# The MLP's down product by one level of Strassen's method, its operands summed in the up stage

## The chip, the cores and the metric

The kernel runs on one core of a Trainium2 chip. The metric is the device time of one execution in microseconds (us); three executions are given, with their median. One further execution was recorded by the hardware profiler, and all rows below are read from it. PE is TensorE, DVE VectorE, ACT ScalarE, POOL GpSimd, SP the sync engine, which here only issues DMAs; POOL issues DMAs too.

## The reference

One step of a small encoder: 1024 prompt frames and 64 sample frames, together T = 1088 columns, model width 1024, two layers. Layer 0 mixes tokens by attention, layer 1 by a gated linear recurrence. Each layer ends with

```python
def sqrelu_mlp(h, w_up, w_down):
    return jnp.square(jax.nn.relu(h @ w_up)) @ w_down
...
        yp = yp + sqrelu_mlp(rmsnorm(yp, mlp_norm[i]), mlp_w_up[i], mlp_w_down[i])
```

where `w_up` is 1024 x 4096 and `w_down` 4096 x 1024, all in float32. After the last layer stands one more rmsnorm.

## The kernel before

Columns are frames. The residual x is held transposed, as four tiles `pair0` to `pair3` of 128 x 2 x 1088 (eight rows of 128 features). A float32 product is made of three matmuls of fp32r operands: each number is split into a high part (a cast) and a low part (the difference), and high x high, high x low and low x high are summed (`product`, L117 to L119). For weights, `parts` makes the two halves: ACT casts (L107), DVE subtracts (L108); a raw weight tile is 128 x 512, that is four blocks of 128 x 128, 256 KB.

Stages in order of time: attention, up and down of layer 0 (`up`, `down`), recurrence, up and down of layer 1, final norm. The PE's order within a stage is written in the code; a scheduler sets the other engines' orders from it, each engine then works its own list strictly in order.

**Up** is already done by a Strassen level in Winograd's form. For each of 16 values of m it makes four pieces of the hidden matrix, 128 rows by half of the columns (544): y11 and y12 are row tile 2m, y21 and y22 are row tile 2m+1, each for the left and the right half of the columns. Seven products of 24 matmuls of 272 columns each (`mul`, L880) give them; weights are combined by `diff` (L925), products by `plus` (L892), `finish` squares (L886, L887) and stores each piece to DRAM (`y_mlp`, L888) through POOL's queue. Before this, the residual itself goes to DRAM (`x_mlp`, L913), so that its four tiles serve as work space.

**Down** takes the 32 hidden tiles in five groups (`GROUPS`), which alternate between two sets of buffers: e (`eh`, `el`, six tiles) and x (`xh`, `xl`, eight tiles). `hidden` loads a tile from `y_mlp` through POOL's queue (L963, 544 KB), ACT casts it (L964), DVE subtracts (L965). The residual comes back by L989 on SP's queue, as do the raw weights (L84). For each group, each of eight output tiles d, and each of three chunks of columns (364, 362, 362; in the last group of layer 1 416, 416, 256), `product` runs over the k tiles of the group and `mix_acc` (L443) adds the result to x.

The pools matter for what follows: the pool `up` holds, among others, the temporaries `d1`, `tt`, `q` and a raw tile of the up stage and is released at its end; the pool `down{layer}` is opened then, in the same memory. A tile of a pool that takes over memory waits until everything that used this memory, DMAs too, is over.

Of the kernel before, what the change touches and what calls it, by code (L numbers as in the profile page):

```python
# [8 lines left out]
F32 = mybir.dt.float32  # L9
# [8 lines left out]
P = 128  # L18
# [10 lines left out]
GROUPS = (4, 8, 6, 8, 6)  # L29
# [10 lines left out]
class Trunk:  # L40
# [717 lines left out]
    def operands(self, gi, ep, up):  # L758
        nc = self.nc
        eh, el = ([ep.tile([P, T], F32R, name=f"e{t}{i}", tag=f"e{t}{i}") for i in range(6)] for t in "hl")  # L760
# [66 lines left out]
    def up(self, ctx, layer, op, up):  # L827
        nc = self.nc
        pu = ctx.enter_context(self.tc.tile_pool(name=f"pu{layer}", bufs=4, space=PSUM))

        def acc():
            return pu.tile([P, 2, 512], F32, name="pu", tag="pu")[:, :, :TH // 2]
# [50 lines left out]
        def finish(t, j, a):  # L883
            y = room("y")
            r = self.rstd[:, TH * j:TH * j + TH]
            nc.vector.scalar_tensor_tensor(cols(y), a, 0.0, cols(r), ALU.max, ALU.mult)  # L886
            nc.scalar.activation(y, y, AF.Square)  # L887
            nc.gpsimd.dma_start(self.yk[layer][t, :, TH * j:TH * j + TH], y)  # L888
# [9 lines left out]
        self.half = None  # L898
# [17 lines left out]
        for t in range(2):  # L916
            for j in range(2):
                finish(t, j, ps[t][j])
# [9 lines left out]
        add, sub = nc.vector.tensor_add, nc.vector.tensor_sub  # L928
        for m in range(1, NF // 2):
# [15 lines left out]
            finish(tb, 1, plus("c", b4, s3))  # L945
            a12 = raw(ta, 1, up)
            mul(b1, self.parts(a12), "b21", True)
            finish(ta, 0, b1)
            mul(b3, self.parts(a22), "t4", True)
            finish(tb, 0, plus("c", b3, s2))  # L950
# [4 lines left out]
    def down(self, ctx, layer, final, ep):  # L955
        nc, tc, A = self.nc, self.tc, self.A
        self.banks(ctx, f"pd{layer}", 8)
        hp = ctx.enter_context(tc.tile_pool(name=f"down{layer}", bufs=1))
        self.CH = CH3

        def hidden(t, hh, hl):
            y = hl[:].bitcast(F32)
            nc.gpsimd.dma_start(y, self.yk[layer][t])  # L963
            nc.scalar.copy(hh[:], y)  # L964
            nc.vector.tensor_sub(hl[:], y, hh[:].bitcast(F32))  # L965
            return hh, hl

        def normed(c, ks):
            s, n = self.CH[c]
            for k in ks:  # L970
                y = hp.tile([P, 416], F32, name="y", tag="y", bufs=4)
# [4 lines left out]
        k0 = 0  # L976
        for g, n in enumerate(GROUPS):
            last = g == len(GROUPS) - 1
            hs = []
            for i in range(n):  # L980
                if g % 2:
                    h = self.xh[i], self.xl[i]
                else:
                    h = (ep.tile([P, T], F32R, name=f"e{t}{i}", tag=f"e{t}{i}") for t in "hl")
                hs.append(hidden(k0 + i, *h))
            if not g:
                self.xp = [self.pair(p) for p in range(4)]
                for p in range(4):
                    nc.sync.dma_start(self.xp[p][:], self.xk[layer][:, 2 * p:2 * p + 2, :])  # L989
            if last:  # L990
                self.new_norm()

            def part(d, into=None):
                return self.weight(A["w_down"][layer, d, :, k0:k0 + n, :], n, into)

            if last and final:
                self.CH, self.big = CHF, hp
                order = (6, 7, 0, 1, 2, 3, 4, 5)
                ws = {d: part(d, [t[i][:, :n * P].rearrange("p (n t) -> p n t", t=P) for t in (self.xh, self.xl)])
                      for d, i in zip(range(KT), order)}  # L1000
                for c in range(3):
                    for d in range(KT):
                        self.mix_acc(ws[d], hs, d, c)
                        done = self.square_part(d, c)
# [169 lines left out]
```

## Time and profile before

| | |
|---|---|
| median of three runs | 2516.59 us (2516.38 to 2516.81) |
| the profiled execution | 2516.2 us |
| its span, first to last instruction | 2514.2 us |
| up of layer 0, down of layer 0 | 397 to 739.6 us, 742.0 to 1124.0 us |
| up of layer 1, down of layer 1 | 1785 to 2114.9 us, 2117.6 to 2501.2 us |
| PE busy | 2471.4 us, 98% of the span |
| DVE, ACT, POOL busy | 59%, 39%, 6% |

The span is 2.0 us shorter than the profiled execution's time. A busy share is one over all stages; the stages differ, so what a change in one of them does has to be read in that stage.

### The profile page before, as it was taken

What the parts mean: (1) busy time and instruction counts of PE and PEld (TensorE: products, weight loads), DVE (VectorE), ACT (ScalarE), POOL (GpSimd) and SP (SyncE); (2) the same over time, 40 slices, a digit from 0 to 9 for tenths busy, and PEclk for the clock granted to TensorE, in tenths of its full rate; (3) what the DMA queues carried; (4) which work ended last, traced back from release to release, by engine and by line L of the source; (5) the groups of instructions that cost most, each with busy time, mean ns of one, the idle gap of its engine ahead of it and who ended that gap; (6) DMA issues with size and microseconds to landing.
All of it is one profiled execution on the core that took longest, in us unless ns stands there. A gap on an engine that the chain in (4) does not pass through costs nothing.

```text
span 2514.2 us, 43600 instructions
## 1 busy us (share of the span) xinstructions
PE 2471.4 (98%) x17704; PEld 2415.7 (96%) x17704; DVE 1485.5 (59%) x2781; ACT 974.3 (39%) x2045; POOL 161.1 (6%) x337
## 2 busy tenths in 40 slices
PE   8999999999999999999999999999999999999998
PEld 7998899999999999999999999999999999999997
DVE  7555458666674243267677777776866667324335
ACT  5236546333342022144555555544633334112122
POOL 2201100101120000000000000000011111000000
PEclk9999999999999999999999999999999999999999
DMA  5322132333363132131111011122233336312211
GB/s 166 85 56 67 38 104 85 108 104 104 104 240 129 43 115 98 42 127 35 38 38 38 29 38 38 32 101 102 92 104 105 104 104 251 104 58 98 104 55 72
DMA packets 108600, 223.39 MB, mean 89 GB/s; under 512 B 29024, under 2 KB 44000, under 8 KB 104672
## 3 DMA queue, kind: packets, MB, share of 16 engines
q1 hardware_dynamic: 85072, 138.84, 17.5%
q0 software_dynamic: 23328, 81.77, 8.8%
q8 instruction: 139, 2.28, 0.4%
q14 instruction: 61, 0.50, 0.1%
HBM read 158.95 MB, written 55.05 MB: 85 GB/s over the span
## 4 chain that ended last, share of the span: by engine, by line
PE 96%; DVE 1%; DMA 1%; ACT 1%; issue 1%; POOL 0%; SPq 0%; POOLq 0%; ACTq 0%; DVEq 0%
PE pu L880 24%; PE mm L117 20%; PE mm L118 19%; PE mm L119 19%; PE sc L331 2%; PE po L365 2%; PE pb L641 2%; PE pu L867 1%; PE pb L605 1%; PE pt L359 1%; PE pb L728 1%; PE pb L700 1%; PE pb L730 1%; PE pb L743 0%; PE pb L672 0%
## 5 line engine op out<-in xcount | busy, mean ns | idle before, releaser
L117 PE MATMUL mm<-xh,whi 128*128 128x384 f32 (+4 forms) x2208 | 731.2, 332 | 14.0 <-ACT whi L107 12.0
L118 PE MATMUL mm<-xl,whi 128*128 128x384 f32 (+4 forms) x2208 | 726.9, 330 | 0.0
L119 PE MATMUL mm<-xh,wlo 128*128 128x384 f32 (+4 forms) x2208 | 724.6, 329 | 0.0
L107 ACT CAST whi<-raw 128x512 fp32r<-128x512 f32 x352 | 197.5, 596 | 655.7 <-PE mm L118 547.8
L117 PEld LDWEIGHTS mm<-xh,whi 128*128 128x128 f32 x2208 | 416.9, 189 | 19.9 <-ACT whi L107 13.0
L443 DVE TENSOR_TENSOR pair<-pair,mm 128x362 f32<-128x362 f32 (+4 forms) x328 | 170.2, 525 | 433.3 <-PE mm L119 431.6
L118 PEld LDWEIGHTS mm<-xl,whi 128*128 128x128 f32 x2208 | 416.7, 189 | 3.5 <-issue 2.2
L119 PEld LDWEIGHTS mm<-xh,wlo 128*128 128x128 f32 x2208 | 416.8, 189 | 3.1 <-issue 1.2
L880 PE MATMUL pu<-xh,wlo 128*128 128x272 f32 x960 | 276.5, 288 | 0.0
L880 PE MATMUL pu<-xl,whi 128*128 128x272 f32 x960 | 275.6, 287 | 0.0
L880 PE MATMUL pu<-xh,whi 128*128 128x272 f32 x960 | 275.5, 287 | 0.0
L108 DVE TENSOR_TENSOR wlo<-raw,whi 128x512 fp32r<-128x512 f32 x352 | 222.5, 658 | 19.1 <-ACT whi L107 18.5
L117 PE MATMUL mm<-eh,whi 128*128 128x362 f32 (+1 forms) x624 | 205.0, 329 | 5.2 <-DVE pair L892 2.8
L880 PE MATMUL pu<-eh,wlo 128*128 128x272 f32 x720 | 208.0, 289 | 0.0
L880 PE MATMUL pu<-eh,whi 128*128 128x272 f32 x720 | 207.6, 288 | 0.4 <-DVE pair L892 0.4
L880 PE MATMUL pu<-el,whi 128*128 128x272 f32 x720 | 206.9, 287 | 0.0
L118 PE MATMUL mm<-el,whi 128*128 128x362 f32 (+1 forms) x624 | 204.7, 328 | 0.0
L892 DVE TENSOR_TENSOR pair<-pu,pair 128x544 f32<-128x544 f32 x150 | 108.5, 723 | 160.4 <-PE pu L880 159.6
L119 PE MATMUL mm<-eh,wlo 128*128 128x362 f32 (+1 forms) x624 | 203.1, 326 | 0.0
L880 PEld LDWEIGHTS pu<-xh,whi 128*128 128x128 f32 x960 | 180.9, 188 | 0.2 <-ACT whi L107 0.2
L880 PEld LDWEIGHTS pu<-xl,whi 128*128 128x128 f32 x960 | 180.5, 188 | 0.0
L880 PEld LDWEIGHTS pu<-xh,wlo 128*128 128x128 f32 x960 | 180.0, 188 | 0.0
(282 smaller groups left out, 4005.5 us busy)
## 6 DMA issues: line engine op xcount, KB each, us to landing
y_mlp<-pair POOLq DMA_DIRECT2D x128, 272.0 KB, 2.4
raw<-in_w_up SPq DMA_DIRECT2D x128, 256.0 KB, 2.7
raw<-in_w_down SPq DMA_DIRECT2D x112, 256.0 KB, 3.0
el<-y_mlp POOLq DMA_DIRECT2D x32, 544.0 KB, 7.2
xl<-y_mlp POOLq DMA_DIRECT2D x32, 544.0 KB, 8.3
raw<-in_w_in SPq DMA_DIRECT2D x64, 256.0 KB, 2.9
x_mlp<-pair SPq DMA_DIRECT2D x8, 1088.0 KB, 5.0
pair<-x_mlp SPq DMA_DIRECT2D x8, 1088.0 KB, 8.7
```

The costliest lines, as they stand in the source:

```text
L107: nc.scalar.copy(hi, raw)
L108: nc.vector.tensor_sub(lo, raw, hi.bitcast(F32))
L117: nc.tensor.matmul(ps[:, :n], wh, ih[:, s:s + n], start=i == 0, stop=False)
L118: nc.tensor.matmul(ps[:, :n], wh, il[:, s:s + n], start=False, stop=False)
L119: nc.tensor.matmul(ps[:, :n], wl, ih[:, s:s + n], start=False, stop=i == last)
L331: nc.tensor.matmul(ps[u][:, i, :kn], st, kd[g][r, k0:k0 + kn], start=True, stop=True)
L359: nc.tensor.transpose(pt[:, kt, :], pb[:, u, kt * P:(kt + 1) * P], self.ident[:])
L365: nc.tensor.matmul(out, ptts[u][:, kt, :], v, start=start, stop=stop)
L443: self.nc.vector.tensor_add(self.x(d)[:, s:s + n], self.x(d)[:, s:s + n], ps)
L641: nc.tensor.matmul(psa[r:r + 64 - hh, i // 2, :].rearrange("p (s t) -> p s t", t=hh), d[:, i * 64:i * 64 + 64 - hh], dv[:, i * ns:(i + 1) ...
L880: nc.tensor.matmul(ps[:, c, :], a, cols(b)[:, c, :], start=not more and p == i == 0, stop=p == 3 and i == 2, skip_group_check=True)
L892: nc.vector.tensor_tensor(t, ps, b, ALU.add)
```

## The change

Down, too, uses one level of Strassen's method. The weight matrix of an output pair m (output tiles 2m and 2m+1) and the hidden matrix are cut in two by rows and columns, b11 to b22 being the hidden quadrants (rows of tiles 2m, 2m+1; left and right columns). Seven products (`PRODS`) each take one combination of weight blocks and one of hidden quadrants and are added to or taken from one or two quadrants of the output. A product runs over all 16 k tiles for four output pairs, in matmuls of 272 columns; per layer 7 x 4 x 16 x 2 x 3 = 2688 matmuls instead of 2304.

The combined operands b21-b11, b21+b22, b11+b22, b12-b22 and b11+b12 are formed in the up stage (`mixed`, five DVE operations of 128 x 544 per m) and stored beside b11 and b22 (`keep`): seven stores of 272 KB per m instead of four. Down then loads 56 hidden tiles of 544 KB per layer instead of 32, forms the weight combination of five of the seven products by DVE (L1010), loads 192 raw weight tiles of 256 KB, and evacuates a product by additions of 128 x 544 (L1030). The PSUM pool of up and down is now one. The new raw tiles of second blocks and the tiles `q` are in `down{layer}` (here `hp`), so in memory that the pool `up` had.

```diff
+PRODS = (
+    (((1, 0), "+", (1, 1)), "b11", ((1, 0, "+"), (1, 1, "-")), ("e0", "e2", "x0", "x2")),
+    (((1, 1),), "b21-b11", ((1, 0, "+"), (0, 0, "+")), ("e4", "x4", "x6", "x0")),
+    (((0, 1), "-", (1, 1)), "b21+b22", ((0, 0, "+"),), ("e0", "e2", "x2", "x4")),
+    (((0, 0), "+", (0, 1)), "b22", ((0, 0, "-"), (0, 1, "+")), ("e4", "x0", "x6", "x2")),
+    (((0, 0), "+", (1, 1)), "b11+b22", ((0, 0, "+"), (1, 1, "+")), ("e0", "e2", "x4", "e4")),
+    (((0, 0),), "b12-b22", ((0, 1, "+"), (1, 1, "+")), ("x0", "x2", "x6", "x4")),
+    (((1, 0), "-", (0, 0)), "b11+b12", ((1, 1, "+"),), ("e0", "e2", "e4", "x0")),
+)
...
+        def mixed(p, f, na, a, sign, nb, b):
+            t = up.tile([P, TH], F32, name="d1", tag="d1", bufs=4)[:]
+            f(t, a, b)
+            self.keep(layer, na + sign + nb, p, t)
...
-            finish(ta, 1, plus("c", b4, s2))
+            y12 = finish(ta, 1, plus("c", b4, s2))
+            mixed(m, sub, "b12", y12, "-", "b22", y22)
+            mixed(m, add, "b11", y11, "+", "b12", y12)
...
+        def load(j, i):
+            (hs, ls), n = pair_of(PRODS[j][3][i])
+            for q, k in enumerate(n):
+                y = ls[k][:].bitcast(F32)
+                nc.gpsimd.dma_start(y, self.yk[layer][j, 2 * i + q].rearrange("p a n -> p (a n)"))
+                nc.scalar.copy(hs[k][:], y)
+                nc.vector.tensor_sub(ls[k][:], y, hs[k][:].bitcast(F32))
+
+        def raw(m, block, i, own):
+            r = self.raw() if own else hp.tile([P, 4, P], F32, name="raw", tag="raw", bufs=3)
+            nc.sync.dma_start(r[:], A["w_down"][layer, 2 * m + block[0], :, block[1], 4 * i:4 * i + 4, :])
+            return r[:]
+
+        def weights(a, m, i):
+            r = raw(m, a[0], i, True)
+            if len(a) > 1:
+                q = hp.tile([P, 4, P], F32, name="q", tag="q", bufs=2)[:]
+                nc.vector.tensor_tensor(q, r, raw(m, a[2], i, False), ALU.add if a[1] == "+" else ALU.subtract)
+                r = q
+            return self.parts(r)
...
+        for j, (a, name, outs, slots) in enumerate(PRODS):
+            end = j == len(PRODS) - 1
+            for m in range(4):
...
+                for i in order:
+                    last = mul(ps, weights(a, m, i), j, i, (0, 1), i == order[0], i == order[-1])
...
+                if j == 0:
+                    self.xp[m] = self.pair(m)
+                    if done:
+                        with tc.issue_after(done.ins):
+                            nc.sync.dma_start(self.xp[m][:], self.xk[layer][:, 2 * m:2 * m + 2, :])
...
+                evacuate(ps, m, outs)
+                if not end and m < 3:
+                    load(j + 1, m)
...
+            if not end:
+                load(j + 1, 3)
```

Where the up stage of layer 0 gives over to down, SP's queue stood as follows; `raw_8089`, `raw_8137` and so on are down's weights, `pair0_8031` to `pair3_8034` the residual, and the names in brackets are the semaphores waited for (DMASW: a DMA issued by POOL; DMAHW: one issued by SP).

```order
L84 DMA raw_8089<-in_w_down 128x512 [waits DMAHW7_49,DVE_49]
L84 DMA raw_8137<-in_w_down 128x512 [waits DMAHW5_49,DVE_49]
L989 DMA pair0_8031<-x_mlp0 128x2176 [waits DMASW3_49,DMASW2_49,DMASW4_49,DMASW1_49,Activation_49]
L84 DMA raw_8185<-in_w_down 128x512 [waits DMAHW1_49,DVE_49]
L989 DMA pair2_8033<-x_mlp0 128x2176 [waits DVE_49]
L84 DMA raw_8233<-in_w_down 128x512 [waits DMAHW4_49,DVE_49]
```

In the changed kernel the same place in SP's queue reads as follows; `raw_8240`, `raw_8272` and `raw_8306` are first blocks, `raw_8243` is the second block that belongs to `raw_8240`, `raw_8275` that of `raw_8272`.

```order
L1003 DMA raw_8272<-in_w_down 128x512 [waits DMAHW0_49,DVE_49]
L883 DMA raw_8101<-in_w_up 128x512 [waits DMAHW6_49,DVE_49]
L1003 DMA raw_8306<-in_w_down 128x512 [waits DMAHW5_49,DVE_49]
L1095 DMA pair0_8372<-x_mlp0 128x2176 [waits DMASW3_49,DMASW4_49,DVE_49,Activation_49]
L1093 DMA pair2_8658<-x_mlp0 128x2176 [waits DVE_49]
L1093 DMA pair3_8801<-x_mlp0 128x2176 [waits DVE_49]
L1093 DMA pair1_8515<-x_mlp0 128x2176 [waits DMASW3_49,DMASW1_49,DMAHW1_49,DVE_49,Activation_49]
L1003 DMA raw_8243<-in_w_down 128x512 [waits DMASW6_49,DMASW5_49,DMASW7_49,DMASW4_49,DMAHW2_49,DMASW3_49,DMAHW4_49,DMASW2_49,DMASW0_49]
L1003 DMA raw_8275<-in_w_down 128x512 [waits DMAHW3_49]
```

The first second block has moved behind all four loads of the residual, and it waits for seven DMAs of POOL's and two of SP's; among them, by their semaphores, are the stores of `d1_8166`, `d1_8169`, `d1_8205` and `d1_8208`, whose memory it takes.

POOL's queue of the changed kernel at this place is the following. `el` and `xl` are hidden tiles that are loaded for products 0 and 1, the `d1` tiles the combined operands of the last m.

```order
L997 DMA xl4_74<-y_mlp0 128x1088
L997 DMA xl5_75<-y_mlp0 128x1088
L997 DMA xl6_76<-y_mlp0 128x1088
L997 DMA xl7_77<-y_mlp0 128x1088
L840 DMA y_mlp0<-d1_8166 128x544
L840 DMA y_mlp0<-d1_8169 128x544
L997 DMA xl3_73<-y_mlp0 128x1088
L840 DMA y_mlp0<-d1_8205 128x544
L840 DMA y_mlp0<-d1_8208 128x544
```

Before, the last two stores of layer 0's up stage stood behind the loads of `xl4` to `xl7` in the same way; now four stores and one more load of a hidden tile stand there.

On DVE the changed kernel has this order ahead of the first weight combination of down, `q_8242`; the rows of line 999 split hidden tiles, and `wlo_8175` is the low part of the first weights of down.

```order
L903 TENSOR_TENSOR d1_8205<-pair1_4582 128x544
L903 TENSOR_TENSOR d1_8208<-pair1_4582 128x544
L999 TENSOR_TENSOR el5_3759<-el5_3759,eh5_3753 128x1088
L999 TENSOR_TENSOR xl4_74<-xl4_74,xh4_66 128x1088
L999 TENSOR_TENSOR xl5_75<-xl5_75,xh5_67 128x1088
L999 TENSOR_TENSOR xl6_76<-xl6_76,xh6_68 128x1088
L999 TENSOR_TENSOR xl7_77<-xl7_77,xh7_69 128x1088
L999 TENSOR_TENSOR xl3_73<-xl3_73,xh3_65 128x1088
L1010 TENSOR_TENSOR q_8242<-raw_8240,raw_8243 128x512
L1010 TENSOR_TENSOR q_8274<-raw_8272,raw_8275 128x512
L118 TENSOR_TENSOR wlo_8175<-q_8242,whi_8174 128x512
```

Before, the first weights of down needed no combination; their cast and subtraction stood among the last operations of the up stage.

## Rows read from the trace of the kernel before

**Rows 1.** The page's head: the span, and busy time of each engine.
```profile
span 2514.2 us, 43600 instructions
PE 2471.4 (98%) x17704; PEld 2415.7 (96%) x17704; DVE 1485.5 (59%) x2781; ACT 974.3 (39%) x2045; POOL 161.1 (6%) x337
```

**Rows 2.** The chain that ended last, by engine (the page's part 4).
```profile
PE 96%; DVE 1%; DMA 1%; ACT 1%; issue 1%; POOL 0%; SPq 0%; POOLq 0%; ACTq 0%; DVEq 0%
```

**Rows 3.** Windows inside up and inside down of layer 0; the first row names columns.
```profile
core 0: us, PE busy (x) PEld busy (x) DVE busy (x) ACT busy (x) POOL busy (x), PEclk, DMA share, GB/s
500.00:600.00 100.00, 100.00 (x800) 100.00 (x800) 62.40 (x96) 33.83 (x58) 10.83 (x20) 1.00 0.32 105
800.00:900.00 100.00, 100.00 (x605) 100.00 (x605) 34.32 (x53) 18.24 (x26) 4.18 (x8) 1.00 0.26 87
```

**Rows 4.** PE's timeline (start, duration, instruction): first and last matmuls of both down stages.
```profile
742.00 0.41 PE L117 MATMUL mm<-eh,whi 128*128 128x364 f32 x1 [2.41 <-ACT pair L887]
...
1123.80 0.32 PE L119 MATMUL mm<-eh,wlo 128*128 128x362 f32 x1
...
2117.64 0.41 PE L117 MATMUL mm<-eh,whi 128*128 128x364 f32 x1 [2.77 <-DVE pair L892]
...
2501.03 0.28 PE L119 MATMUL mm<-eh,xl 128*128 128x256 f32 x1
```

**Rows 5.** Groups of instructions by form: of up 425:739, the last of down 745:1120.
```profile
L892 DVE TENSOR_TENSOR pair<-pu,pair 128x544 f32<-128x544 f32 x74 | 53.5, 724 | 79.6 <-PE pu L880 79.0
L107 ACT CAST whi<-q 128x512 fp32r<-128x512 f32 x29 | 17.9, 618 | 15.1 <-PE pu L880 15.1
L925 DVE TENSOR_TENSOR q<-raw 128x512 f32<-128x512 f32 x14 | 9.7, 692 | 9.7 <-DMA raw<-in_w_up 9.7
...
L965 DVE TENSOR_TENSOR el<-el,eh 128x1088 fp32r<-128x1088 f32 x12 | 15.4, 1288 | 4.1 <-ACT eh L964 3.9
```

**Rows 6.** Windows after up of layer 0 (columns as in Rows 3).
```profile
740.00:745.00 5.00, 3.00 (x18) 3.03 (x19) 5.00 (x7) 4.25 (x6) 1.61 (x3) 1.00 1.02 418
755.00:760.00 5.00, 5.00 (x32) 5.00 (x31) 2.76 (x4) 2.21 (x2) 0.00 (x0) 1.00 0.77 307
```

**Rows 7.** The tile y_mlp in 745:748: the last store of layer 0's up stage.
```profile
L888 POOL DMA_DIRECT2D y_mlp<-pair x1: 552/552/552, 745.8 to 745.8; - x1
...
DMA to landing us min/median/max: 14.5/14.5/14.5
```

**Rows 8.** The same in 2121:2124, the last store of layer 1's up stage.
```profile
DMA to landing us min/median/max: 14.7/14.7/14.7
```

**Rows 9.** DMA issues over the whole span: KB each, median us to landing.
```profile
y_mlp<-pair POOLq DMA_DIRECT2D x128, 272.0 KB, 2.4
raw<-in_w_down SPq DMA_DIRECT2D x112, 256.0 KB, 3.0
```

**Rows 10.** PE's timeline at the start of the program.
```profile
12.00 0.69 PE L117 MATMUL mm<-xh,whi 128*128 128x384 f32 x1 [12.00 <-ACT whi L107]
...
13.21 0.52 PE L117 MATMUL mm<-xh,whi 128*128 128x384 f32 x1
13.53 0.52 PE L118 MATMUL mm<-xl,whi 128*128 128x384 f32 x1
...
17.63 0.34 PE L118 MATMUL mm<-xl,whi 128*128 128x384 f32 x1
17.80 0.34 PE L118 MATMUL v<-xl,whi 128*128 128x384 f32 x1
```

**Rows 11.** The window at the start of layer 0's up stage (columns as in Rows 3).
```profile
397.00:425.00 28.00, 27.70 (x214) 27.41 (x215) 25.42 (x43) 18.98 (x33) 1.09 (x2) 1.00 0.24 89
```

**Rows 12.** PE's first matmul of the recurrence, behind down of layer 0.
```profile
1124.84 0.41 PE L117 MATMUL mm<-xh,whi 128*128 128x384 f32 x1 [0.71 <-DVE pair L443]
```

**Rows 13.** SP's DMA queue in 742:757: packets, MB, share of 16 engines.
```profile
q1 hardware_dynamic: 502, 2.61, 42.4%
```

**Rows 14.** The same queue in 742:750.
```profile
q1 hardware_dynamic: 212, 1.23, 37.0%
```

**Rows 15.** Weight raw tile issued at 743.7, in 743:744: us from issue to landing.
```profile
DMA to landing us min/median/max: 9.2/9.2/9.2
```

More of the change, by code (lines that the diff above doesn't have):

```diff
@@ L825, in operands, with keep, up @@
         return Ops()
[L827 removed]
+    def keep(self, layer, name, p, t):
+        i = [n for _, n, _, _ in PRODS].index(name)
+        self.nc.gpsimd.dma_start(self.yk[layer][i, p // 2, :, p % 2, :], t)
+    def up(self, layer, op, up, acc):
         nc = self.nc
[L829 to L832 removed]
         def cols(t):
@@ L956, in down, with pair_of @@
         nc, tc, A = self.nc, self.tc, self.A
[L957 to L966, printed above, removed]
+        self.CH = CH4
+        def pair_of(slot):
+            i = int(slot[1])
+            return [(self.eh, self.el) if slot[0] == "e" else (self.xh, self.xl)][0], (i, i + 1)
@@ new lines, in weights, with mul @@
+        def weights(a, m, i):
[5 more added lines that the diff above has]
+            return self.parts(r)
+        def mul(ps, w, j, i, cs, first, last):
+            (hs, ls), n = pair_of(PRODS[j][3][i])
+            for k in range(4):
+                t, o = n[k // 2], TH * (k % 2)
+                for c in cs:
+                    s = slice(o + TH // 2 * c, o + TH // 2 * c + TH // 2)
+                    for x, (a, b) in enumerate(((0, hs), (0, ls), (1, hs))):
+                        done = nc.tensor.matmul(ps[:, c, :], w[k][a], b[t][:, s], start=first and k == x == 0,
+                                                stop=last and k == 3 and x == 2)
+            return done
@@ L974, in normed @@
                 nc.sync.dma_start(self.O["y"][:, k, s:s + n], y[:, :n])
[L976 to L990, printed above, removed]
-                self.new_norm()
[L993 to L1004, printed above, removed]
-                        if c and d == 2:
-                            self.scaled(c - 1)
-                            normed(c - 1, (range(KT), range(3))[c - 1])
-                self.scaled(2)
-                with tc.issue_after(done.ins):
-                    normed(1, range(3, KT))
-                    normed(2, range(KT))
-                return
-            for d in range(KT):
-                w = part(d)
-                for c in range(3):
-                    self.mix_acc(w, hs, d, c)
-                if last:
-                    for c in range(3):
-                        self.scale_part(2, d, c)
-                        if d:
-                            self.square_part(d - 1, c)
-            k0 += n
@@ L1026, in mlp @@
+        scale(7, H1)
     def mlp(self, layer, wa, wb, na, final):
@@ L1035, in mlp, with acc @@
                     self.mix_rest(wa, wb, op, na)
-                with ExitStack() as c3:
-                    self.up(c3, layer, op, up)
+                pu = ctx.enter_context(tc.tile_pool(name=f"pu{layer}", bufs=4, space=PSUM))
+                def acc():
+                    return pu.tile([P, 2, 512], F32, name="pu", tag="pu")[:, :, :TH // 2]
+                self.up(layer, op, up, acc)
             with ExitStack() as c2:
-                self.down(c2, layer, final, ep)
+                hp = c2.enter_context(tc.tile_pool(name=f"down{layer}", bufs=1))
+                self.down(layer, final, hp, acc)
     def run(self):
```

108 lines of the change are left out of this document (91 added, 17 removed).

## The prediction

> **What bounds the kernel now.** I read the page's head first: PE is busy for 98% of the span [rows 1], and the chain that ended last is PE's for 96% [rows 2]. So a stage costs what its matmuls cost, unless something makes PE wait. The windows inside the two stages of the MLP then give the price of a matmul. In up, 100 us hold 800 matmuls of 272 columns, 0.125 us each; in down 605 of 362 or 364 columns, 0.165 us each. PE is busy for all of both windows, DVE for 62% and 34%, and the DMA share is 0.32 and 0.26 [rows 3]. So there is slack beside PE in both, more in down. The third thing to read is the seam between up and down. There PE stands for only 2.4 us in layer 0 and 2.8 us in layer 1 [rows 4], while the DMA engines are full (share 1.02) and stay full until about 758 us, some 19 us after PE ended the up stage [rows 6]. I call the end of the up stage's last matmul T; it is 739.6 us in layer 0 (742.00 less the idle 2.41). The last store of the up stage is issued at T + 6.2 and lands 14.5 us later, at T + 20.7; in layer 1 that takes 14.7 us [rows 7, 8]. Today nobody on PE's side waits for that landing.
>
> **The change, part by part.** *Matmuls of down.* The stages run from 742.00 to 1123.96 and from 2117.64 to 2501.15, start of the first matmul to start of the last plus one spacing, 765.5 us together [rows 4]. The new ones have 2 x 2688 matmuls of 272 columns. At the up stage's 0.125 us, the same shape with the same triple of splits, that is 672.0 us. Gain: 93.5 us, if nothing makes PE wait.
>
> *The seam.* The first down product needs the sum of two weight blocks. The second block, `raw_8243`, is loaded into memory that the up stage's `d1` tiles had, and those are being stored. The rows of SP's queue show the wait: this load waits for the stores of `d1_8208` and its three companions, behind all residual loads. Everything of down's weights is behind it: `q_8242` on DVE, the cast on ACT, PE. When does the last store land? Before, the last store landed at T + 20.7 behind a full set of DMAs. Now three more stores of m = 15 (0.84 MB), two of m = 14 that are still in flight (0.56 MB), and the residual's fourth load (1.11 MB), which was later, share this stretch, while some 1.0 MB of weight loads leave it. Net 1.5 MB at the 418 GB/s that the full engines moved [rows 6] are 3.6 us: T + 24.3. The two extra sums on DVE put its issue 1.4 us later, which a full queue hides. Then the weight load takes 3.0 us [rows 9] in a queue that has just emptied, the sum on DVE 0.69, the cast on ACT 0.62 [rows 5], and I allow 0.3 for the hand-offs: PE restarts at T + 28.9. Today it restarts at T + 2.4 and T + 2.8, so the seams cost 26.5 + 26.1 = 52.6 us. Bounds: if the store found an empty queue it would land 2.4 us after its issue at T + 7.6 [rows 9], and PE would restart at T + 14.6, 24 us in all; if the last store came at T + 28 and the weight load took the 9.2 us of a full queue [rows 15], it would be T + 38.8, 72 us. I take the middle value, since the store's row at the very place is 14.5 us and not 2.4.
>
> *The restart.* After 12 us without work at the program's start, matmuls of 384 columns follow one another every 0.32 us, which is the 1.2 GHz level of TensorE's clock, until 17.63 us; from then on every 0.17 [rows 10]. These 17 matmuls took 5.6 us where 2.9 were due at 0.172: 2.7 us. After the 2.4 us at the seam today no such stretch follows [rows 4, 6]. PE will now stand for more than twice 12 us, so I charge 2.7 us per seam, 5.4 us.
>
> *Inside up.* Five sums of 0.724 us [rows 5] per m, in 21 us, add 17% to DVE's 62% and three stores of 0.28 MB per m add 40 to 105 GB/s [rows 3]. PE has its weights by then; I charge nothing for the steady part. At the start DVE is busy for 25.4 of 28 us [rows 11], and five more sums (3.6 us) stand there ahead of the operands and weights of m = 1. Between 0 and 1.8 us per layer; 1 each, 2 us in all.
>
> *Inside down.* A product lasts 384 x 0.125 = 48 us. DVE needs for a two-block product 16 sums and 16 low parts at 0.69, 8 evacuations at 0.72 and 8 hidden tiles at 1.29 [rows 5]: 38 us, 80%, against 34% today [rows 3]. SP's queue brings 32 raw tiles, 8.4 MB, 175 GB/s; POOL's 8 hidden tiles, 4.5 MB. On average that is 268 of 418 GB/s, but the hidden tiles come together when a product ends and their buffers fall free. While both queues were full, SP's carried 2.61 MB in 15 us, 174 GB/s [rows 13], and in the first 8 us of this 154 [rows 14]. So weights just keep pace during a burst, with a landing that grows from 3.0 to 9.2 us [rows 9, 15], against two blocks of weights in hand, 48 matmuls or 6 us. I take 0.4 us for each of twelve ends of products, 5 us; the bounds are 0 and 3.5 us each.
>
> A rule of the Trainium skill, page "DMA: Bandwidth & Descriptors", section "Queues, rings and completion order", says that each engine takes turns between the queues that have work, a packet at a time. By equal turns of equal packets SP would have half of 418, 209 GB/s, enough for 175, and the 5 us would be nothing (2484 us); the two windows above show less than half, and the measurement decides here.
>
> *The end of down.* The recurrence's first matmul waits 0.7 us today [rows 12]; the new last evacuation is 544 columns wide (0.72 us, [rows 5]) and the shared PSUM pool is released only then: 1 us more. The final norm is unchanged but for a fourth chunk; nothing.
>
> Sum, against the profiled execution's 2516.2 us, 0.4 below the median: 2516.2 - 93.5 + 52.6 + 5.4 + 2 + 5 + 1 = 2488.7. Forecast: 2489 us, some 1.1% faster. More than half of what the matmuls give goes back at the two seams.
>
> **The rivals.** *The seam is short.* If the last stores land early, near T + 10 to T + 16, the seam costs 8 to 14 us less per layer than above: 2460 to 2472 us. For it: the stores are small, and the memory is theirs alone to release. Against it: POOL's queue lands in order, the last store of today lands a few us behind the loads ahead of it, and now one more load stands ahead.
>
> *The seam is longer.* The weight load goes out behind a still full queue: up to 10 us more per layer, 2503 to 2509 us. Against it: the stores are among the last of the burst.
>
> *Weights starve in down; this is the one that ends slower.* Each product begins with the burst of hidden tiles. If SP's queue gets r GB/s then, the burst lasts 4460 / (418 - r) us, and PE loses the share 1 - r/175 of it. At the 154 of rows 14 that is 2 us per end, 25 us over twelve ends in place of 5: 2509 us. It is slower than before by 0.2% (about what a measurement can tell from no change; 2521.6 us) from 3.1 us per end on, that is below 141 GB/s, or if the first late landing adds to it. For it: 80% of DVE, whose list is strictly in order, so that a hidden tile that is late stands before a weight sum that is not; only 6 us of weights in hand. Against it: two of seven products need one block only, and 174 GB/s over the longer window.
>
> *The change gives no shorter matmuls.* The spacing of 0.125 us holds in up only with 62% of DVE beside it; but PE was busy throughout there, and the shape is the same. I give this no chance of its own.
>
> **How the numbers follow.** Likeliest, as summed, 0.50, with a range of its own of 2474 to 2503 us (12 us of seam and 3 of stalls either way). Short seam 0.15. Longer seam 0.12. Starvation 0.23, of which 0.08 above 2521.6, 0.06 between 2511 and 2521.6, and the rest below. Faster by over 0.2% therefore 0.86, within 0.2% 0.06, slower 0.08. A range of 2460 to 2513 us leaves out what would lie below the short seam's bound and the upper part of starvation, somewhat under 2 in 10.
>
> **What the changed profile would show.** The down windows away from ends of products should hold 800 matmuls in 100 us. PE's list of waits should begin with two idle times of about 26 to 30 us before the first matmul of down, in each case released by the cast of the first weights, and the chain there should run from a store of `y_mlp` over a load of `raw` and the DVE sum to the cast. The first 3 to 6 us after should show half the pace. Idle times at ends of products should be below 1 us, with raw landings of up to 9 us. I am wrong if the seam's idle time is below 18 or above 36 us, if PE waits in the middle of products for `whi` or `wlo`, or if the up stage has become longer by more than 3 us.

## The result, and the profile after

The changed kernel takes 2487.93 us (median of four runs, 2486.93 to 2492.47), the kernel before 2516.7 (2516.38 to 2521.87); the ratio is 0.9884, with an interval of 0.9867 to 0.9902. The forecast was 2489. The profiled execution took 2486.93 us, its span is 2485.2. Line numbers are those of the changed kernel: up's matmuls are now L891, down's L1021, the casts of weights L117.

The page's head, to be laid beside [rows 1], shows that PE's share has fallen and DVE's has risen from 59% to 70%:

```profile
span 2485.2 us, 46519 instructions
PE 2389.9 (96%) x18474; PEld 2334.2 (94%) x18474; DVE 1747.8 (70%) x3120; ACT 1079.4 (43%) x2200; POOL 238.9 (10%) x481
```

PE's list of waits (us in total, times, longest) has one new item at its head, one wait per layer; before, PE stood at the two seams for 2.4 and 2.8 us [rows 4]:

```profile
PE pu L1021 <- ACT whi L117: 56.4, 2, 28.3
```

PE's timeline (start, duration, instruction) gives the stages, as [rows 4] did: the last matmul of up and the first of down in layer 0, three of the slow start, the first two at full pace, down's last matmul in layer 0, and down's first and last in layer 1.

```profile
738.05 0.29 PE L891 MATMUL pu<-xh,wlo 128*128 128x272 f32 x1
766.47 0.59 PE L1021 MATMUL pu<-eh,whi 128*128 128x272 f32 x1 [28.13 <-ACT whi L117]
...
769.12 0.43 PE L1021 MATMUL pu<-eh,whi 128*128 128x272 f32 x1
769.35 0.43 PE L1021 MATMUL pu<-el,whi 128*128 128x272 f32 x1
769.58 0.43 PE L1021 MATMUL pu<-eh,wlo 128*128 128x272 f32 x1
...
770.44 0.29 PE L1021 MATMUL pu<-eh,whi 128*128 128x272 f32 x1
770.56 0.29 PE L1021 MATMUL pu<-el,whi 128*128 128x272 f32 x1
...
1108.00 0.29 PE L1021 MATMUL pu<-eh,wlo 128*128 128x272 f32 x1
...
2127.19 0.59 PE L1021 MATMUL pu<-eh,whi 128*128 128x272 f32 x1 [28.28 <-ACT whi L117]
...
2471.54 0.29 PE L1021 MATMUL pu<-eh,wlo 128*128 128x272 f32 x1
```

From these and [rows 4], between starts of first and last matmuls: down has become shorter by 40.3 us in layer 0 (381.80 to 341.54) and 39.0 in layer 1 (383.39 to 344.35), 79.3 together. The seams have become longer, from start to start, by 25.7 and 25.5 us (2.70 and 3.05 before), 51.2 together. The two up stages are 1.7 us shorter (layer 1's stage before begins at 1771.5 us; the table ahead of the prediction has 1785). What comes ahead of the first up stage is 0.9 us shorter, the stretch between the layers 1.2 longer, the tail 0.5 longer. That is the whole span's 29.0 us: 79.3 - 51.2 + 1.7 - 0.8.

The chain that ends with the first weights of down in layer 0 names each step of the seam; each row is a start, a duration and what ran. (The load and the sum in it are those of the second pair of blocks, whose sum stands on DVE ahead of the first low part; the first pair's load took 2.9 us.)

```profile
737.26 11.51 DMA xl<-y_mlp
...
748.81 0.49 issue
749.30 12.47 DMA y_mlp<-d
...
762.42 3.58 DMA raw<-in_w_down
766.00 0.02 issue
766.02 0.69 DVE q L1010
766.72 0.61 DVE wlo L118
```

Read as the forecast reads it (766.47 less the idle 28.13), the up stage's last matmul ends at T = 738.3. The last store is issued at 749.30, T + 11.0 (its turn on POOL's queue came when the load of `xl4` landed), and lands at 761.77, T + 23.4. Weight loads follow at once, then the sum. A second thing can be read on DVE at the same place: its list holds the last hidden tile of the seam until 762.8, two microseconds before the first sum.

```profile
761.52 1.29 DVE L999 TENSOR_TENSOR xl<-xl,xh 128x1088 fp32r<-128x1088 f32 x1 [1.32 <-ACT xh L998]
765.02 0.69 DVE L1010 TENSOR_TENSOR q<-raw 128x512 f32<-128x512 f32 x1 [2.21 <-DMA raw<-in_w_down]
```

So two holds ran side by side, and the one by memory ended last, by some 2 us.

The windows (columns as in [rows 3]) show the seam and the steady stages: a granted clock of 0.50 where PE stands still, with the DMA engines full at 750 us and at 0.38 behind 760; then up with DVE at 78% and still 800 matmuls in 100 us, and down with 795.

```profile
745.00:750.00 5.00, 0.00 (x0) 0.00 (x0) 3.36 (x5) 2.16 (x2) 1.08 (x2) 0.50 1.01 419
...
760.00:765.00 5.00, 0.00 (x0) 0.00 (x0) 1.49 (x2) 1.10 (x1) 0.00 (x0) 0.50 0.38 105
...
500.00:600.00 100.00, 100.00 (x800) 100.00 (x800) 77.62 (x119) 34.32 (x59) 18.98 (x35) 1.00 0.41 144
...
900.00:1000.00 100.00, 100.00 (x795) 100.00 (x795) 73.23 (x105) 38.95 (x57) 8.48 (x16) 1.00 0.76 261
```

### The profile page after: what moved, and what is told of

Read it like the earlier page. It is cut to its first block, busy times and chain, and to the rows that moved or that the text cites. A ratio compares the mean times of both kernels' runs of the same rounds, so it can differ in the third digit from the quotient of the medians.

```text
span 2485.2 us, 46519 instructions
## 1 busy us (share of the span) xinstructions
PE 2389.9 (96%) x18474; PEld 2334.2 (94%) x18474; DVE 1747.8 (70%) x3120; ACT 1079.4 (43%) x2200; POOL 238.9 (10%) x481
## 4 chain that ended last, share of the span: by engine, by line
PE 73%; issue 17%; DMA 4%; POOL 3%; DVE 2%; ACT 1%; POOLq 0%; SPq 0%; DVEq 0%; ACTq 0%
PE pu L1021 18%; PE pu L891 13%; PE mm L127 10%; PE mm L129 9%; PE mm L128 9%; POOL y_mlp L840 2%; PE sc L341 2%; PE po L375 2%; PE pb L651 2%; PE pu L878 1%; DMA xl<-y_mlp 1%; DMA y_mlp<-d 1%; DMA raw<-in_w_down 1%; PE pb L615 1%; PE pt L369 1%
## 5 line engine op out<-in xcount | busy, mean ns | idle before, releaser
L127 PE MATMUL mm<-xh,whi 128*128 128x384 f32 (+2 forms) x1440 | 478.9, 333 | 13.9 <-ACT whi L117 11.7
L128 PE MATMUL mm<-xl,whi 128*128 128x384 f32 (+2 forms) x1440 | 474.7, 330 | 0.0
L129 PE MATMUL mm<-xh,wlo 128*128 128x384 f32 (+2 forms) x1440 | 473.5, 330 | 0.0
L1021 PE MATMUL pu<-xh,wlo 128*128 128x272 f32 x1024 | 296.4, 289 | 0.5 <-DVE wlo L118 0.3
L1021 PE MATMUL pu<-xh,whi 128*128 128x272 f32 x1024 | 296.0, 289 | 0.5 <-DVE pair L1030 0.5
L1021 PE MATMUL pu<-xl,whi 128*128 128x272 f32 x1024 | 295.7, 289 | 0.0
L117 ACT CAST whi<-raw 128x512 fp32r<-128x512 f32 (+1 forms) x288 | 166.4, 608 | 261.6 <-PE mm L128 92.0
L1021 PE MATMUL pu<-eh,whi 128*128 128x272 f32 x768 | 224.3, 292 | 56.4 <-ACT whi L117 56.4
L891 PE MATMUL pu<-xh,wlo 128*128 128x272 f32 x960 | 276.6, 288 | 0.0
L891 PE MATMUL pu<-xl,whi 128*128 128x272 f32 x960 | 275.6, 287 | 0.0
L891 PE MATMUL pu<-xh,whi 128*128 128x272 f32 x960 | 275.4, 287 | 0.0
L117 ACT CAST whi<-q 128x512 fp32r<-128x512 f32 x220 | 130.6, 618 | 279.7 <-PE pu L1021 187.6
L118 DVE TENSOR_TENSOR wlo<-raw,whi 128x512 fp32r<-128x512 f32 (+1 forms) x288 | 187.5, 673 | 62.4 <-ACT whi L117 61.9
L1021 PE MATMUL pu<-eh,wlo 128*128 128x272 f32 x768 | 224.0, 292 | 0.1
L1021 PE MATMUL pu<-el,whi 128*128 128x272 f32 x768 | 223.5, 291 | 0.0
L891 PE MATMUL pu<-eh,wlo 128*128 128x272 f32 x720 | 208.0, 289 | 0.0
L891 PE MATMUL pu<-eh,whi 128*128 128x272 f32 x720 | 207.5, 288 | 0.0
L891 PE MATMUL pu<-el,whi 128*128 128x272 f32 x720 | 207.0, 287 | 0.0
```

Source lines behind the costliest of these rows:

```text
L117: nc.scalar.copy(hi, raw)
L118: nc.vector.tensor_sub(lo, raw, hi.bitcast(F32))
L127: nc.tensor.matmul(ps[:, :n], wh, ih[:, s:s + n], start=i == 0, stop=False)
L128: nc.tensor.matmul(ps[:, :n], wh, il[:, s:s + n], start=False, stop=False)
L129: nc.tensor.matmul(ps[:, :n], wl, ih[:, s:s + n], start=False, stop=i == last)
L891: nc.tensor.matmul(ps[:, c, :], a, cols(b)[:, c, :], start=not more and p == i == 0, stop=p == 3 and i == 2, skip_group_check=True)
```

## The experiments

Each was timed beside the kernel before on the same chip; ratios are to that. The kernel before had medians of 2515.7 to 2517.8 us there.

**Up's share alone.** The kernel before, with the five sums and three more stores per m:

```diff
-            finish(ta, 1, plus("c", b4, s2))
+            y12 = finish(ta, 1, plus("c", b4, s2))
+            mixed(m, sub, 1, y12, y22)
+            mixed(m, add, 2, y11, y12)
```

> The kernel before with only the up stage's share of the change: five sums per m on DVE, three of them stored besides the four pieces (nobody reads them; down is the old one). The forecast charged 2 us in all, at the start of up, and nothing for DVE at 80% and 145 GB/s in the steady part: 2516 to 2521 us, up windows with 800 matmuls in 100 us. If the sums delay the operands or weights of up, the up stages get longer by 3 us or more each: above 2523 us.

2514.05 us, ratio 0.9988 (0.9979 to 0.9998): no loss. The window 500:600 has DVE at 79% and no matmul fewer:

```profile
500.00:600.00 100.00, 100.00 (x801) 100.00 (x800) 78.82 (x121) 33.55 (x58) 18.88 (x35) 1.00 0.41 143
```

The first-to-last time of the up stages is 342.8 and 343.0 us against 342.0 and 343.05 before. The sums are free where they stand, and in all of up they cost at most 0.8 us. What the change loses, it loses after up.

**Own memory for the second blocks.** The pool `up` stays open and down uses its raw and sum buffers (the final norm's temporary tiles move to that pool too, four in place of six):

```diff
-            r = self.raw() if own else hp.tile([P, 4, P], F32, name="raw", tag="raw", bufs=3)
+            r = self.raw() if own else hp.tile([P, 4, P], F32, name="raw", tag="raw", bufs=2)
...
-            with ExitStack() as c2:
-                hp = c2.enter_context(tc.tile_pool(name=f"down{layer}", bufs=1))
-                self.down(layer, final, hp, acc)
+                self.down(layer, final, up, acc)
```

> The second weight blocks and their sums take the two raw and two q buffers of the up stage (which are free early) in place of new memory under the stores' buffers; nothing else is changed, except that there are two second blocks in flight and not three. If the wait for the landing of the last stores is what sets the seam, the first weights are ready soon after the up stage, PE restarts after 3 to 5 us of idle time, and stands a second time, 6 to 9 us, for the hidden tile xl3 that is loaded late: 9 to 14 us per layer in place of 28.1, and 2449 to 2462 us. If it is the full DMA engines whatever waits are named, the weights come as late as before: idle time over 20 us and 2475 to 2488 us. If two buffers are too few for down, PE shows waits for whi or wlo all through the stage.

2460.56 us, ratio 0.9768 (0.9753 to 0.9782). The wait of 28 us is gone. In layer 0 (735 to 1098 us) PE's waits are:

```profile
PE pu L1021 <- DVE wlo L118: 4.8, 3, 3.7
PE pu L1021 <- ACT whi L117: 3.7, 2, 3.0
PE pu L1021 <- ACT xh L998: 1.8, 1, 1.8
```

With a fourth of 0.3 they sum to 10.6 us, and all lie before 770 us; the one for `xh` is the late hidden tile. Two buffers in place of three cost nothing that shows. But the edit does more than its diff says: with the weights free early, the scheduler also put the first weight sum ahead of twelve hidden tiles on DVE that had stood before it. So this run ends both holds, and doesn't tell them apart. It does set aside one rival: the DMA engines were as full as in the change (share 1.03 in 735:745), and the first weights came in time all the same. What is left at this place is DVE: it has no free moment from 740 to 755 us; these two windows show the last 10 us of that.

```profile
745.00:750.00 5.00, 1.16 (x8) 0.72 (x6) 5.00 (x8) 3.36 (x4) 1.53 (x3) 0.85 1.04 424
750.00:755.00 5.00, 4.42 (x19) 4.42 (x20) 5.00 (x7) 2.25 (x3) 0.64 (x2) 0.50 1.01 407
```

The second window also has a granted clock of 0.50 while PE works, after waits of 0.7 and 3.7 us. The short waits therefore cost more than their length: layer 0's down takes 18.6 us more than its matmuls at full pace, of which only 10.6 are waits, and 105 of both layers' down matmuls come at the slow pace of 0.20 to 0.26 us, against 34 in the change.

**The last stores ahead of product 1's tiles**, the memory wait kept:

```diff
+                if j == 0 and m < 3:
+                    with tc.issue_after(self.kept.ins):
+                        load(1, m)
```

> The change as it is, but the six hidden tiles of product 1 that stood ahead of the last stores in POOL's queue are queued behind them; no wait is removed. If the seam is set by the landing of the last store and that by the bytes ahead of it (3.3 MB less at 418 GB/s, 8 us), the last store lands about 15 us after the up stage, the weight load takes 5 to 9 us behind the hidden tiles, and the idle time is 20 to 25 us: 2472 to 2484 us. If the place in the queue doesn't matter, 28 us and 2488 us.

2494.82 us, ratio 0.9902 (0.9882 to 0.9922): no faster than the change, against the expectation (the intervals of the two overlap, so slower isn't shown by the times). PE's idle time is 30.6 us per layer. The stores did land earlier: SP's first weight load goes out at 756.11, 17 us after the up stage. But the chain now runs through the hidden tiles, which DVE's list holds ahead of the sum:

```profile
750.44 15.34 DMA xl<-y_mlp
...
766.98 0.04 DVE xl L999
...
768.19 0.68 DVE q L1010
```

The second hold had moved to the front. The edit itself helped it there: it puts these tiles' loads behind the stores, so that the last of them lands at 765.8 us.

**Both edits.** 

> Both edits. If the memory wait and the late hidden tile are the two things that hold the seam, one behind the other, the idle time falls to 3 to 8 us per layer: 2436 to 2450 us. If the full DMA engines are the true cause, the weights starve instead, more than 15 us per layer: above 2465 us.

2465.83 us, ratio 0.9788 (0.9773 to 0.9803): 5 us above own memory alone by the medians, which the intervals don't separate. PE waits 14 us in layer 0 (735 to 1100 us), 8.4 of them for `whi`. Product 1's tiles now land while product 0 already runs; that the weights are late because they share the engines with them is likely, but no run shows it. Neither of the two expectations fits well; the size is that of the second.

**Hidden tiles of products 1 to 6 behind the weights on SP's queue**, the memory wait kept:

```diff
-                nc.gpsimd.dma_start(y, self.yk[layer][j, 2 * i + q].rearrange("p a n -> p (a n)"))
+                (nc.sync if j else nc.gpsimd).dma_start(y, self.yk[layer][j, 2 * i + q].rearrange("p a n -> p (a n)"))
...
-                if not end and m < 3:
-                    load(j + 1, m)
+                if not end and m < 3:
+                    with tc.issue_after(self.got.ins):
+                        load(j + 1, m)
```

> The change as it is, memory wait included, but the hidden tiles of products 1 to 6 are loaded by SP's queue, each pair of tiles behind the weights of the output pair before, so that none of product 1's is loaded, cast or subtracted at the seam. If the run with the stores first came out no better because DVE's and ACT's lists held those tiles ahead of the first weight sum, the idle time is now the landing of the last store (17 us after the up stage there) plus a weight load in an empty queue, 3 us, plus 1.6: 20 to 23 us per layer, 2472 to 2480 us. If the landing of the last store doesn't depend on what stands ahead, 28 us and 2488 us.

The seam is as expected, the whole is not: 2506.35 us, ratio 0.9964 (0.9952 to 0.9977). PE's waits over the span (the profiled execution was the slowest of nine, 2514.35 us):

```profile
PE pu L1021 <- ACT whi L117: 53.8, 13, 21.9
PE pu L1021 <- DVE wlo L118: 15.4, 19, 0.9
```

The longest are now the seams, 21.9 and 21.2 us: this is what the memory wait alone costs when nothing of product 1 stands there. The chain of layer 0 has the same steps as the change's (a store that lands at 756.0, a load of 3.1 us, the sum, the cast), and DVE's last hidden tile ahead of the sum was done at 751.8. The others are new. A hidden tile of 544 KB on SP's queue stands before weights that PE needs next, throughout down. Full engines alone don't explain them: the DMA share from 800 to 1050 us is 0.68. POOL's queue in the change as it is keeps these apart.

**The same with own memory.** 

> Own memory for the second blocks and sums, and the hidden tiles of products 1 to 6 behind the weights on SP's queue. If the memory wait and the crowd of hidden tiles at the seam are the two causes, and both are gone, PE stands for 3 to 8 us in all per seam: 2438 to 2452 us. If instead the weights starve in a DMA queue that is full anyway (residual, stores, product 0's tiles), there are waits for whi and wlo of over 12 us per layer and 2460 us or more. Later in down the loads are spread, so that ends of products should show nothing new; if hidden tiles now stand before weights on one queue, waits of over 1 us appear there.

2482.67 us, ratio 0.9867 (0.985 to 0.9883). The seams are short (7 us of waits each), but there are 26 waits for `wlo` and 9 for `whi`, 36 us in all, most of them later in down. That is the last sentence of the expectation, and more of it than I had thought.

**Only product 1's tiles on SP's queue**, own memory: `nc.sync if j == 1 else nc.gpsimd`, and the ordering for product 1 alone.

> Own memory, and only product 1's hidden tiles behind the weights on SP's queue; those of products 2 to 6 stay on POOL's. If the run with all of them on SP's queue lost its gain because a hidden tile stands before weights there at each end of a product, this one keeps its short seam (5 to 8 us) and has no waits later: 2446 to 2456 us, faster than own memory alone. If loading product 1's tiles within product 0 starves the weights wherever they are queued, it is no faster than own memory alone, 2458 to 2466 us.

2449.37 us, ratio 0.9733 (0.9719 to 0.9748): 9 us (by the ratios) to 11 us (by the medians) better than own memory alone, and, with the last version below, the fastest that computes the whole result. In layer 0 PE waits 7.7 us (735 to 1092 us), all but one wait of 1.0 us (at 804) within the first 36 us of down:

```profile
PE pu L1021 <- DVE wlo L118: 6.6, 5, 3.7
PE pu L1021 <- ACT whi L117: 1.1, 2, 0.7
```

One of them, of 1.5 us up to 773.9, is followed by slow matmuls and this window:

```profile
775.00:780.00 5.00, 5.00 (x30) 5.00 (x30) 1.90 (x4) 1.98 (x3) 0.00 (x0) 0.68 1.00 367
```

**Last m's sums on GpSimd**: `add, sub = nc.gpsimd.tensor_add, nc.gpsimd.tensor_sub` for the last m, for these five sums alone.

> As the run before, with the five sums of the last m (a fifteenth part of the change's sums) done by GpSimd. DVE was busy without a break from 740 to 755 us in the run with own memory, and PE waited 3.7 us there for wlo. If DVE's crowd at the seam sets that wait, it falls by 2 to 3.5 us per layer: 4 to 7 us faster than the run before. If the weights' transfers set it, no change.

2460.19 us, ratio 0.9774 (0.9755 to 0.9793): 11 us worse. GpSimd needs 1.74 us for a sum, DVE 0.72 [rows 5], and its queue of transfers stands still meanwhile; PE waits 11.8 us in layer 0 in place of 7.7. The wait for `wlo` of 3.7 us became 4.2. One more thing is in this trace: while GpSimd sums, DVE's own operations take far longer. The split of a hidden tile takes 2.41 us and the low part of a weight tile 1.90, against 1.28 and 0.68 in the run before:

```profile
749.89 2.41 DVE L1001 TENSOR_TENSOR xl<-xl,xh 128x1088 fp32r<-128x1088 f32 x1
752.22 1.90 DVE L118 TENSOR_TENSOR wlo<-q,whi 128x512 fp32r<-128x512 f32 x1
```

So moving the sums took no load off DVE, and this run says nothing on what DVE's crowd costs.

**No tiles of product 1.** Own memory; the loads and splits of the first six hidden tiles of product 1 are left out.

> Own memory, with the first six hidden tiles of product 1 neither loaded nor split (that product then works on what the up stage left there). Nothing of them is left at the seam, neither bytes nor DVE and ACT work: the bound of what any order of these loads can give. If they are what delays PE after the memory wait is gone, PE's waits at the seam fall from 10 us to below 5 per layer: 2444 to 2452 us. If the residual, the stores and the up stage's own tail delay it, 2456 to 2462 us.

2443.92 us, ratio 0.9706 (0.9687 to 0.9726). PE's waits in layer 0 fall from 10.6 to 6.1 us, the 3.7 for `wlo` among them as before. Hence product 1's tiles cost own memory some 16 us of the whole, and loading them behind the weights on SP's queue gets back 9 to 11 of these. About half of the 16 us are waits; most of the rest is clock: 51 of down's matmuls have the slow pace here, against 105 with own memory.

The wait of 3.7 us that remains isn't theirs, and DVE's list shows what makes it. The cast `whi` is done at 746.0; DVE then works without a break on two hidden tiles and two sums, and only then on the low part:

```profile
745.38 0.62 ACT L117 CAST whi<-q 128x512 fp32r<-128x512 f32 x1 [0.79 <-DVE q L1010]
745.90 1.28 DVE L999 TENSOR_TENSOR xl<-xl,xh 128x1088 fp32r<-128x1088 f32 x1
747.11 1.35 DVE L903 TENSOR_TENSOR d<-pair 128x544 f32<-128x544 f32 x2
748.38 1.28 DVE L999 TENSOR_TENSOR xl<-xl,xh 128x1088 fp32r<-128x1088 f32 x1
749.58 0.68 DVE L118 TENSOR_TENSOR wlo<-q,whi 128x512 fp32r<-128x512 f32 x1
```

The run with the sums on GpSimd took the two sums out of this list, at the price shown above.

**Keeping PE busy through the seam.** 54 float32 matmuls that nobody reads stand between up and down of the changed kernel:

```diff
+        fill = acc()
+        for n in range(54):
+            nc.tensor.matmul(fill[:, n % 2, :], self.ones[:], self.rstd[:, TH // 2 * (n % 2):TH // 2 * (n % 2) + TH // 2],
+                             start=True, stop=True)
```

> The change as it is, with 54 float32 matmuls of 272 columns (ones by the row scale, into a PSUM tile that nobody reads) between up and down, some 25 us of work for PE that is not part of the computation. No wait is changed. If the slow first matmuls after the seam come from PE having stood still, they now follow one another every 0.125 us from the first on and the time is 4 us less, 2484 us; the idle time before the first matmul of down is 2 to 4 us, and it starts no earlier. If they are slow because their operands come late, nothing changes: 2488 us.

2488.18 us, ratio 0.9887 (0.9873 to 0.9902), no change; the slow start is there again. But the fill ended at 762.5, and PE then stood still for 3.6 us:

```profile
766.06 0.39 PE L1021 MATMUL pu<-eh,whi 128*128 128x272 f32 x1 [3.57 <-ACT whi L117]
...
767.18 0.43 PE L1021 MATMUL pu<-eh,whi 128*128 128x272 f32 x1
767.41 0.43 PE L1021 MATMUL pu<-el,whi 128*128 128x272 f32 x1
```

With 61 of them:

> The fill between up and down with 61 matmuls in place of 54, so that it reaches up to the first matmul of down; with 54 PE stood still for another 3.6 us and the slow stretch was there again. If standing still is the cause, the first matmuls of down now follow one another every 0.126 us, and the span is 2 us per seam shorter than the change's, if the fill doesn't end too late; if late operands are the cause, the slow stretch is there as before.

2483.72 us, ratio 0.9862 (0.9845 to 0.9878); the span is 2481.9 us against 2485.2. The intervals of this run and of the change overlap, so the matmuls decide and not the times. The fill lasts to within 0.4 us of the weights in layer 0, and the pace is full from the fourth matmul on:

```profile
767.33 0.40 PE L1021 MATMUL pu<-eh,whi 128*128 128x272 f32 x1 [0.42 <-ACT whi L117]
767.57 0.28 PE L1021 MATMUL pu<-el,whi 128*128 128x272 f32 x1
768.06 0.39 PE L1021 MATMUL pu<-eh,wlo 128*128 128x272 f32 x1 [0.21 <-DVE wlo L118]
768.29 0.29 PE L1021 MATMUL pu<-eh,whi 128*128 128x272 f32 x1
768.42 0.29 PE L1021 MATMUL pu<-el,whi 128*128 128x272 f32 x1
```

So the slow start comes from standing still, not from late operands, which are there in both runs (waits of 0.2 us for `wlo`). Layer 1 agrees: with 54, PE stood for 3.4 us and the slow stretch came, though only after ten matmuls; with 61 it stood for 1.9 us and no slow stretch followed. Counted in all of down, 34 matmuls of the change have the slow pace of 0.20 to 0.26 us, with this fill 7.

**Columns innermost.** The fastest version, with the loop over the two halves of columns inside the one over high and low parts.

> The run with product 1's tiles on SP's queue, with the two halves of columns innermost: the two matmuls of one pair of operands (say high by high) follow one another and share their weights. Down's matmuls came every 0.1261 us in every version, up's every 0.1253, a difference that took some 4 us of the gain. If it comes from the order in which weights and operands alternate, the spacing changes, either way by 0.5 ns or more: 2.7 us or more in all; if not, 0.1261 as before and 2449 us.

2449.85 us, ratio 0.9736 (0.9718 to 0.9754): the same time. The mean spacing of down's matmuls at full pace fell from 126.10 to 125.48 ns, so the order matters, and by the size expected; 799 and not 796 matmuls lie in the window 900:1000. In 800:900 there are 766 and not 785: waits of 1.1 and 0.8 us lie there now (one of 1.0 in the version it was made from), and the granted clock is 0.98.

```profile
800.00:900.00 100.00, 98.03 (x766) 97.58 (x765) 62.36 (x83) 38.15 (x53) 8.48 (x16) 0.98 0.67 230
900.00:1000.00 100.00, 100.00 (x799) 100.00 (x798) 74.37 (x106) 43.04 (x63) 9.01 (x17) 1.00 0.78 266
```

## Why the prediction was right, point by point

**Matmuls of down.** The gain of 93.5 us was too high by 5.9: the new matmuls come every 0.1261 us and not every 0.125, 5376 times. Of the 1.1 ns, 0.3 are up's own: its mean spacing before is 0.1253 us, which the forecast took as 0.125 from 800 matmuls in 100 us. The last experiment shows that the order of weights and operands carries 0.6. It isn't the DMA load: within the changed kernel's down the spacing is 126.06 ns where the DMA share is below 0.4 and 126.11 where it is above 0.95. The remaining 0.2 ns are open.

**The seam.** This was the term that decided, and it holds: 51.2 us for the forecast's 52.6. Store, weight load, sum and cast came in the order given. The landing at T + 23.4 was forecast as T + 24.3, the first weight load took 2.9 us and not 3.0, and PE restarted at T + 28.1 in place of 28.9. The store was issued at T + 11.0, 3.4 us later than the forecast's T + 7.6; as POOL's stores landed one after another right behind the tiles ahead of them (760.4, then 761.1 and 761.8), that made no difference, as the forecast said of its own 1.4 us. One thing the forecast didn't price, though the orders shown ahead of it contain it, is the second hold: DVE's list, as it stood, would have kept the sum until 762.8 us even with the memory free. The run with the stores first shows such a hold at work, the one with the loads behind the weights the memory wait without it. Against a shorter seam the forecast said that the store lands behind what is queued ahead of it; the run with the stores first confirms it, since the landing came some 6 us earlier with six tiles less in front.

**The restart.** Charged with 5.4 us. In layer 0 the first 15 steps of down took 4.0 us where 1.9 were due at 0.126, in layer 1 the first 23 steps 5.4 where 2.9 were due: 2.1 and 2.5, 4.6 in all. The mechanism is shown by the two fills, 54 and 61.

**Inside up.** Charged with 2 us; the run with up's share alone shows at most 0.8, and the stages of the changed kernel are 1.7 us shorter, for a reason that stays open. The charge was wrong, and it was small.

**Inside down.** Charged with 5 us for twelve ends of products, out of bounds of 0 and 42; 3.6 us are left there beside pace and restart, most of them in layer 1's norm. In the profile after PE has no wait of 0.6 us or more before the last output pair of layer 1, so the bursts of hidden tiles are hidden almost altogether. But the forecast's way to its 5 us was wrong in two steps, and they cancel. It took SP's share of a full DMA from [rows 13, 14], stretches over which the two queues did not take turns throughout (27 packets of SP's against 217 of POOL's in 742:744, 64 against 63 in 746:748). Around the end of product 1 in the changed kernel, with weights on SP's queue and hidden tiles on POOL's, the window 864:872 has

```profile
q0 software_dynamic: 577, 2.23, 68.9%
q1 hardware_dynamic: 577, 1.05, 34.3%
```

The first number counts packets: it is the same for both queues. That is the rule which the forecast weighed (the Trainium skill, page "DMA: Bandwidth & Descriptors", section "Queues, rings and completion order": each engine takes turns between the queues with work, a packet at a time), and this trace agrees with it. But the packets are not equal, 1.8 KB on the mean for weights and 3.9 KB for hidden tiles, so SP got 131 GB/s: not 209, not 174, and less than the 141 below which the rival with starving weights was to be slower than before. PE didn't wait all the same. What fits this, though no run tested it, is the blocks of weights in hand, which the forecast named and that rival's formula left out. By an estimate from these rows, the eight hidden tiles of a product (4.46 MB at 279 GB/s) keep both queues full for 16 us; at 44 GB/s short of 175 the weights then lack 0.7 MB, 1.3 blocks of 0.52 MB, and two are in hand. So the small charge was right by luck, and weights come nearer to starving here than the forecast had it. The runs with hidden tiles on SP's queue don't test this: what they lost, 18 us of the whole although the two seams became 13 us shorter, they lost with a DMA share of 0.68 (in the first of them).

**The end of down** was charged with 1 us. The recurrence starts 0.16 us later behind the last matmul, and the tail after layer 1's down is 0.5 us longer. That down is 2.8 us longer than layer 0's: 0.4 of restart, and for the most part the norm's own matmuls and a wait of 0.5 us that lie between its matmuls.

So the errors partly cancel. Against the sum of 2488.7, the profiled execution has 5.9 us more for the matmuls, and less for the seam (1.4), the restart (0.8), up (2 charged, 1.7 gained: 3.7), stalls in down (3.6 for 5: 1.4) and the rest (0.4): 2486.9. The forecast's error is smaller than its terms' errors, and that much of its closeness is luck; the seam, which decided, was right by its mechanism.

## What to carry to other kernels

Where a pool takes over the memory of another, look for what still leaves the old one: a store that nobody needs soon becomes the wait of the first load that everybody needs, at the price of the whole DMA queue ahead of that store. Freeing the memory isn't enough: read what stands before the first use on each engine in order (here hidden tiles for the next product before the first weight sum), since the next hold may end only microseconds earlier. Transfers that are needed at once and transfers that are needed later are best kept on different queues; moving the later ones behind the urgent ones on one queue helped at the seam (9 to 11 us for product 1's tiles alone) and, done throughout down, lost more than that. When two full queues share the engines, compare the sizes of their packets before their bytes: here the queue with the small packets got a third.

## What the runs showed of the hardware

TensorE's pace after standing still: 2.4 us of idle time left it at full speed (the seam before), and so did 1.9 us (61 fills, layer 1); 3.6 us were followed by matmuls of 272 columns every 0.227 us, that is 1.2 GHz, for about a dozen matmuls (54 fills), and so were 28 us. After the 28 us the price was 2.1 and 2.5 us. The length of one wait doesn't settle it: with product 1's tiles on SP's queue a wait of 1.5 us was followed by a granted clock of 0.68 in the next 5 us, and with own memory short waits left 105 slow matmuls. In the windows the granted clock reads 0.50 in the idle time of the seam.

Matmuls of one size, 272 columns, at full pace came every 125.3 ns on the mean in up, 126.1 in down and 125.5 in down with the columns innermost: the order in which weights and operands alternate is worth half a per cent.

Two DMA queues that both had work moved the same number of packets (577 and 577 in 8 us), so that their bytes went by packet size: 1.05 and 2.23 MB.

GpSimd took 1.74 us for a sum of 128 x 544 that takes DVE 0.72, and a weight tile's low part on DVE beside it took 1.90 us in place of 0.68.
